# Compression's first layer as three f16 products a step, with keys and values split ahead of their copies

## The chip, the cores and the metric

The kernel runs on one core of a Trainium2 chip. The metric is the device time of one execution in microseconds (us), from the start of the program to its end; lower is better. A core has five engines with instruction queues of their own, each worked off in order: TensorE (PE in the profile, its weight loads PEld), VectorE (DVE), ScalarE (ACT), GpSimd (POOL) and SyncE (SP, which here only issues transfers). Transfers run on 16 DMA engines.

## The reference, cut to what matters

The program computes two transformer blocks for 256 tokens of width 1024. In the first block one branch is a sparse attention, which also attends to *compressed* keys and values: every 16 tokens a window of 32 tokens, with a position vector added to each token, is flattened and passed through a small two-layer network, once for keys (j = 0) and once for values (j = 1), in both groups g of heads:

```python
n_cmp = (T - CMP_BLOCK) // CMP_STRIDE + 1          # 15 windows
def compress(kx, j):
    blk = kx[:, :, cmp_idx] + pe_cmp[j]            # 32 tokens x 64
    flat = blk.reshape(B, G, n_cmp, CMP_BLOCK * dh)    # 2048 long
    return jax.nn.silu(flat @ w_cmp1[j]) @ w_cmp2[j]   # 2048 -> 128 -> 64
```

The change concerns `flat @ w_cmp1[j]`, a product of 2 x 15 rows of length 2048 with a 2048 x 128 matrix, for j = 0 and 1.

## The kernel before, in words

Nearly all products are made with numbers split in two f16 halves: a weight chunk of 1 MB arrives as f32 in a tile `raw` (pool `wraw`, four buffers), ACT writes its rounded half (`hi`, L194) and DVE the rest (`lo`, L195) into a tile `whl` (three buffers), in two steps of 128x1024 each, and PE adds up hi x hi, hi x lo and lo x hi (L215 to L217 where the weights are stationary, L236 to L238 where the activations are).

Compression's first layer is the exception: it is made in f32. `kv_pair(0, kvc)` (L472) writes keys and values of all tokens to `kvc` (ACT, L468, two instructions). The tile `k2` (L480, slot G23) is cleared by a DVE memset (L481), and four GpSimd transfers (L483, L484) lay the rows of `kvc` into it, for each group once as they are and once moved by one token, so that the 128 partitions hold two tokens of 64 values. A third plane of `k2` takes the position vectors, which two SyncE transfers (L563) write into every second element, 4 bytes at a time. The first-layer weights `w1` come by SyncE (L565) as 1 MB each, straight into two tiles `thg` of f32. A step k (L497) multiplies a 128x128 block of `w1` with 45 columns of `k2` (15 windows of two groups and 15 of the plane of position vectors), and 16 steps add up one j. `compress` (L502) then adds the column of the position vectors to the others (L504, L505), applies the nonlinearity and makes the second layer.

The order around it in the program's text: projection of keys and values (`kv_pair(0)`), queries 0 and 1 (`nq_pair(0)`, L561), the loads of position vectors and `w1` (loop at L562), queries 2 and 3 (`nq_pair(2)`), the other keys (`kv_pair(2, ksw)`, L568), then `projB('vsw', ...)` (L583), which makes a projection in 16 rounds of three matmuls and calls `two_steps` (L577) ahead of each round: two compression steps a round, 32 in all. An explicit edge (`issue_after`) keeps them behind `kv_op`, the last matmul of `kv_pair(2)`. After that come `compress` for both j, and the attention.

The kernel doesn't write out the queues' order otherwise: the framework lays the instructions of each engine out when it compiles, by the program's order and by what it thinks is ready, and adds the waits. So ACT's queue has work of later lines ahead of work of earlier ones (for instance squares of `memT`, L356, ahead of L468). Tiles with the same tag share a slot: the next user waits for the last reader. `e8` (L452), a small table that goes out by a GpSimd transfer (L455, `edr`), has the slot of `kvc`, so L468 waits for that transfer. The PSUM tiles `mm_ps` have two buffers, so `nq_pair(2)` can start only when L468 has emptied that of `kv_pair(0)`.

Of the kernel before, what the change touches and what calls it, by code (L numbers as in the profile page):

```python
# [8 lines left out]
F32 = mybir.dt.float32  # L9
F16 = mybir.dt.float16  # L10
I32 = mybir.dt.int32
AF = mybir.ActivationFunctionType
OP = mybir.AluOpType
# [4 lines left out]
T = 256  # L18
# [4 lines left out]
SW = 512.0  # L23
# [53 lines left out]
def trunk_kernel(ctx, tc, ap, off, dump=None):  # L77
    nc = tc.nc
    V, S, PE, G = nc.vector, nc.scalar, nc.tensor, nc.gpsimd
# [4 lines left out]
    wraw = ctx.enter_context(tc.tile_pool(name="wraw", bufs=4))  # L84
    wsp = ctx.enter_context(tc.tile_pool(name="wsp", bufs=3))
    act = ctx.enter_context(tc.tile_pool(name="act", bufs=1))
# [347 lines left out]
    nc.sync.dma_start(out=rows, in_=bass.AP(tensor=r_ap.tensor, offset=r_ap.offset, ap=[[0, 128], [1, NROW]]))  # L434
    smw = act.tile([128, 608], F32, name="smw", tag="Y").rearrange("p (k c) -> p k c", k=8)
    nc.sync.dma_start(out=smw, in_=ap['wsm'])
    smh = const.tile([128, 8, 56], F16, name="smh")
    sml = const.tile([128, 8, 56], F16, name="sml")
    split(smw[:, :, :56], smh, sml, SW)
# [37 lines left out]
    wc2 = const.tile([128, 2, 64], F32, name="wc2")  # L477
    nc.sync.dma_start(out=wc2, in_=ap['wcmp2'])
    cw1 = []
    k2 = act.tile([128, 2, 3, 272], F32, name="k2", tag="G23")  # L480
    V.memset(k2, 0.0)  # L481
    for g, gp in enumerate((slice(0, 64), slice(64, 128))):
        G.dma_start(out=k2[0:64, :, g, :T], in_=kvc[gp])  # L483
        G.dma_start(out=k2[64:128, :, g, :T - 1], in_=kvc[gp, :, 1:])  # L484
    ck2 = [k2[:, j] for j in range(2)]
    bt = act.tile([128, 8, T], F32, name="bt", tag="Q8")
    G.dma_start(out=bt, in_=bass.AP(tensor=edr.tensor, offset=edr.offset, ap=[[1, 128], [384, 8], [1, T]]))

    def compress_step(j):

        ps = sm_ps()[:, :45].rearrange("p (g c) -> p g c", g=3)
        k_ = [0]

        def step():
            k = k_[0]
            k_[0] += 1
            PE.matmul(ps, cw1[j][:, k * 128:k * 128 + 128], ck2[j][:, :, 2 * k:2 * k + 225:16],  # L497
                      start=k == 0, stop=k == 15)

        return ps, step  # L500

    def compress(j, ps):  # L502
        z = sm.tile([128, 45], F32, name="cz").rearrange("p (g c) -> p g c", g=3)
        V.tensor_copy(z[:, 2, 0:1], ps[:, 2, 0:1])  # L504
        V.tensor_scalar(z[:, 0:2], ps[:, 0:2], z[:, 2, 0:1], None, op0=OP.add)  # L505
        th = sm.tile([128, 2, 15], F32, name="cth")
        S.activation(out=th, in_=z[:, 0:2], func=AF.Tanh, scale=0.5)
        if j == 0:
            hd = sm.tile([128, 2, 15], F32, name="chd")
            V.scalar_tensor_tensor(hd, th, 1.0, z[:, 0:2], op0=OP.add, op1=OP.mult)  # L510
            ps = sm_ps()
# [48 lines left out]

    nq_pair(0)  # L561
    for j in range(2):  # L562
        nc.sync.dma_start(out=ck2[j][:, 2, 0:32:2], in_=ap['pe'][j])  # L563
        w1 = gpool.tile([128, 8, T], F32, name="thg").rearrange("p k t -> p (k t)")
        nc.sync.dma_start(out=w1, in_=ap['wc1'][j])  # L565
        cw1.append(w1)
    nq_pair(2)
    kv_op = kv_pair(2, ksw)  # L568
# [1365 lines left out]
```

## Time and profile before

| | |
|---|---|
| median of 3 runs | 917.85 us (914.5 to 918.71) |
| the profiled execution: time | 914.95 us |
| the profiled execution: span on the core | 913.2 us |
| TensorE busy | 885.0 us, 97% of the span |
| VectorE busy | 698.3 us, 76% |
| ScalarE busy | 539.1 us, 59% |
| GpSimd busy | 53.1 us, 6% |

The span is the time between the first and the last recorded instruction; 1.75 us of the execution lie around it. Each row of the timeline gives start, duration, engine, line and operation, output and inputs, shapes, and in brackets how long the engine was idle just before and what ended that. Matmuls are pipelined: the duration of one is its way through the array, and the rate at which they are worked off is read from the distance of their starts.

### The profile page before, as it was taken

To read this page: it belongs to the slowest core of one execution; us is meant where nothing else is said; L and a number is where in the kernel's file an instruction comes from. 1 tells how busy PE (TensorE), PEld (TensorE's weight loads), DVE (VectorE), ACT (ScalarE), POOL (GpSimd) and SP (SyncE) were. 2 spreads that over 40 slices of the span, in tenths; PEclk is the share of its full clock that TensorE was granted. 3 is DMA by queue.
4 is the path that set the end of the run, shared out by engine and by line. 5 is a ranking of instruction groups with operands and counts; after the bars stand their busy time and mean duration, and the time that the engine had idled before them with its cause. 6 is when DMAs were issued, how large, how long until landed. Compare 5 with 4: busy or idle time off the path is not lost. (4 is left out here: it accounts for less than half of the span.)

```text
span 913.2 us, 21140 instructions
## 1 busy us (share of the span) xinstructions
PE 885.0 (97%) x8843; PEld 758.1 (83%) x8843; DVE 698.3 (76%) x1484; ACT 539.1 (59%) x924; POOL 53.1 (6%) x61
## 2 busy tenths in 40 slices
PE   8899999999999999999999999999999999999995
PEld 6787687998888888888888888888888988777773
DVE  8768897767887667557998988767644888899994
ACT  7575947655565454444655765574345656597871
POOL 1310000000200000012000010000001000001102
PEclk9999999999999999999999999999999999999998
DMA  9881355365565565555545243456554666899991
GB/s 331 298 276 72 105 185 184 117 208 185 185 208 208 190 211 201 188 205 186 186 139 186 94 146 133 139 188 224 189 184 134 246 235 220 305 365 415 409 404 34
DMA packets 33331, 189.86 MB, mean 208 GB/s; under 512 B 7571, under 2 KB 7996, under 8 KB 11724
## 3 DMA queue, kind: packets, MB, share of 16 engines
q1 hardware_dynamic: 31004, 178.43, 54.6%
q0 software_dynamic: 2192, 9.97, 3.3%
q8 instruction: 71, 1.16, 0.5%
q14 instruction: 32, 0.26, 0.1%
q10 hardware_dynamic: 32, 0.03, 0.0%
HBM read 185.86 MB, written 2.37 MB: 206 GB/s over the span
## 5 line engine op out<-in xcount | busy, mean ns | idle before, releaser
L195 DVE SCALAR_TENSOR_TENSOR whl<-raw,whl 128x1024 f16<-128x1024 f32 (+1 forms) x264 | 313.2, 1210 | 68.8 <-ACT whl L194 67.2
L194 ACT ACTIVATE whl<-raw 128x1024 f16<-128x1024 f32 (+1 forms) x264 | 261.7, 1029 | 104.8 <-issue 51.6
L215 PE MATMUL mm_ps<-u,whl 128*128 128x256 f16 x792 | 216.6, 274 | 2.9 <-ACT whl L194 2.9
L217 PE MATMUL mm_ps<-u,whl 128*128 128x256 f16 x792 | 216.6, 273 | 0.9 <-DVE whl L195 0.9
L216 PE MATMUL mm_ps<-u,whl 128*128 128x256 f16 x792 | 216.6, 273 | 0.0
L215 PEld LDWEIGHTS <-whl 128*128 128x128 f16 x1768 | 174.7, 99 | 24.2 <-ACT whl L194 3.2
L217 PEld LDWEIGHTS <-whl 128*128 128x128 f16 x1768 | 173.3, 98 | 22.9 <-DVE whl L195 1.1
L216 PEld LDWEIGHTS <-whl 128*128 128x128 f16 x1768 | 173.3, 98 | 21.9 <-issue 1.8
L216 PE MATMUL mm_ps<-f,whl 128*128 128x256 f16 x352 | 95.9, 273 | 0.0
L217 PE MATMUL mm_ps<-f,whl 128*128 128x256 f16 x352 | 95.9, 273 | 0.0
L215 PE MATMUL mm_ps<-f,whl 128*128 128x256 f16 x352 | 95.9, 273 | 0.0
L998 ACT ACTIVATE gu_t<-mm_ps 128x256 f32<-128x256 f32 x22 | 8.5, 384 | 53.8 <-PE mm_ps L217 53.8
L236 PE MATMUL mm_ps<-whl,u 128*128 128x256 f16 x128 | 35.1, 275 | 0.0
L238 PE MATMUL mm_ps<-whl,u 128*128 128x256 f16 x128 | 34.9, 272 | 0.0
L237 PE MATMUL mm_ps<-whl,u 128*128 128x256 f16 x128 | 34.8, 272 | 0.0
L999 DVE SCALAR_TENSOR_TENSOR gu_t<-gu_t,mm_ps 128x256 f32<-128x256 f32 x22 | 9.2, 420 | 31.2 <-ACT gu_t L998 31.2
L338 POOL TENSOR_TENSOR sqa<-sqa,sq 128x512 f32<-128x512 f32 x8 | 13.8, 1728 | 306.5 <-ACT sq L356 306.4
L1751 PEld LDWEIGHTS <-ehid 128*80 128x80 f16 x132 | 14.6, 117 | 13.5 <-ACT ehid L294 2.0
L1705 PEld LDWEIGHTS <-whl 128*128 128x128 f16 x576 | 21.6, 100 | 3.5 <-issue 1.8
L215 PE MATMUL mm_ps<-mg,whl 128*128 128x256 f16 x64 | 17.4, 272 | 0.3 <-ACT mg L294 0.3
L216 PE MATMUL mm_ps<-mix,whl 128*128 128x256 f16 x64 | 17.4, 272 | 0.2 <-DVE mix L298 0.2
L215 PE MATMUL mm_ps<-mix,whl 128*128 128x256 f16 x64 | 17.1, 272 | 0.4 <-DVE gtmp L898 0.4
(610 smaller groups left out, 1836.2 us busy)
## 6 DMA issues: line engine op xcount, KB each, us to landing
raw<-in_w SPq DMA_DIRECT2D x138, 1024.0 KB, 4.9
raw_G<-in_w SPq DMA_DIRECT2D x9, 1024.0 KB, 6.6
raw_R<-in_w SPq DMA_DIRECT2D x5, 1024.0 KB, 7.3
raw_Y<-in_w SPq DMA_DIRECT2D x5, 1024.0 KB, 10.8
raw_K<-in_w SPq DMA_DIRECT2D x4, 1024.0 KB, 12.5
raw<-in_w SPq DMA_DIRECT2D x7, 512.0 KB, 7.4
thg<-in_wc SPq DMA_DIRECT2D x2, 1024.0 KB, 11.3
whl<-in_w POOLq DMA_DIRECT2D x2, 1024.0 KB, 9.7
```

Of the source, the lines that this page charges most:

```text
L194: S.activation(out=hi[:, p], in_=raw[:, p], func=AF.Copy, scale=SW)
L195: V.scalar_tensor_tensor(lo[:, p], raw[:, p], SW, hi[:, p], op0=OP.mult, op1=OP.subtract)
L215: PE.matmul(out, wh, xh[:, k0 + k], start=first and k == 0, stop=False)
L216: PE.matmul(out, wh, xl[:, k0 + k], start=False, stop=False)
L217: i = PE.matmul(out, wl, xh[:, k0 + k], start=False, stop=last and k == nk - 1)
L236: PE.matmul(ps[:, a, :w], xh[:, k, ts], hv[:, k], start=k == 0, stop=False)
L237: PE.matmul(ps[:, a, :w], xh[:, k, ts], lv[:, k], start=False, stop=False)
L238: PE.matmul(ps[:, a, :w], xl[:, k, ts], hv[:, k], start=False, stop=k == 7)
L338: self.eng.tensor_tensor(out=acc, in0=acc, in1=sq, op=OP.add)
L999: V.scalar_tensor_tensor(th, th, 1.0, ps[:, :T], op0=OP.add, op1=OP.mult)
L1705: unit_op[0] = PE.matmul(o, w_[:, b], xg[x_][:, g, k], stop=x_ == 1 and k == 7, start=w_ is hi and x_ == 0 and k == 0)
L1751: PE.matmul(dps[c], hh[:, x_, k], w_[:, k * D + c * 512:k * D + c * 512 + 512], start=e % 4 == 0 and k == 0 and i == 0, stop=e % 4 == 3 an ...
```

## The change

Each number of `kvc`, of the position vectors and of `w1` is split in an f16 half and a rest, and each compression step becomes three f16 matmuls (hi x hi, hi x lo, lo x hi) in place of one of f32, which the trace shows as two instructions. The weights' hi and lo are scaled by SW = 512, and `compress` takes the scale out. The splits are made by `split`: ACT writes hi (L294), DVE the rest (L296 for scale 1, L298 otherwise). `kvc` is split once, ahead of the four copies, into `kv16` (slot pct); the copies then move hi and lo of both j. `k2` is now f16, twice as many elements of half the size, and lies in slot K8 (next used by `xp`). The position vectors come in one transfer early in the program, contiguous, to a tile of their own, and are split into `k2`. `w1` arrives in the pool `wraw`, and four splits of 128x1024 write it into `thg`.

```diff
+    pe32 = sm.tile([128, 2, 16], F32, name="pe32", bufs=1)
+    nc.sync.dma_start(out=pe32, in_=ap['pe'].rearrange("j p c -> p j c"))
...
-    k2 = act.tile([128, 2, 3, 272], F32, name="k2", tag="G23")
+
+    kv16 = act.tile([128, 2, 2, T], F16, name="kv16", tag="pct")
+    split(kvc, kv16[:, 0], kv16[:, 1], 1.0)
+    k2 = act.tile([128, 2, 2, 3, 272], F16, name="k2", tag="K8")
     V.memset(k2, 0.0)
+    split(pe32, k2[:, 0, :, 2, 0:32:2], k2[:, 1, :, 2, 0:32:2], 1.0)
+    k2_ = k2.rearrange("p s j g t -> p (s j) g t")
+    kv_ = kv16.rearrange("p s j t -> p (s j) t")
     for g, gp in enumerate((slice(0, 64), slice(64, 128))):
-        G.dma_start(out=k2[0:64, :, g, :T], in_=kvc[gp])
-        G.dma_start(out=k2[64:128, :, g, :T - 1], in_=kvc[gp, :, 1:])
-    ck2 = [k2[:, j] for j in range(2)]
+        G.dma_start(out=k2_[0:64, :, g, :T], in_=kv_[gp])
+        G.dma_start(out=k2_[64:128, :, g, :T - 1], in_=kv_[gp, :, 1:])
...
-            PE.matmul(ps, cw1[j][:, k * 128:k * 128 + 128], ck2[j][:, :, 2 * k:2 * k + 225:16],
-                      start=k == 0, stop=k == 15)
+            for i, (w_, x_) in enumerate(((0, 0), (0, 1), (1, 0))):
+                PE.matmul(ps, cw1[j][:, w_, k * 128:k * 128 + 128], k2[:, x_, j, :, 2 * k:2 * k + 225:16],
+                          start=k == 0 and i == 0, stop=k == 15 and i == 2)
...
-        V.tensor_copy(z[:, 2, 0:1], ps[:, 2, 0:1])
-        V.tensor_scalar(z[:, 0:2], ps[:, 0:2], z[:, 2, 0:1], None, op0=OP.add)
+        V.tensor_scalar(z[:, 2, 0:1], ps[:, 2, 0:1], 1.0 / SW, None, op0=OP.mult)
+        V.tensor_scalar(z[:, 0:2], ps[:, 0:2], 1.0 / SW, z[:, 2, 0:1], op0=OP.mult, op1=OP.add)
...
     for j in range(2):
-        nc.sync.dma_start(out=ck2[j][:, 2, 0:32:2], in_=ap['pe'][j])
-        w1 = gpool.tile([128, 8, T], F32, name="thg").rearrange("p k t -> p (k t)")
-        nc.sync.dma_start(out=w1, in_=ap['wc1'][j])
+        raw = wraw.tile([128, 2048], F32, name="raw")
+        nc.sync.dma_start(out=raw, in_=ap['wc1'][j])
+        w1 = gpool.tile([128, 8, T], F32, name="thg").bitcast(F16).rearrange("p k t -> p (k t)")
+        w1 = w1.rearrange("p (s c) -> p s c", s=2)
+        for i in range(2):
+            split(raw[:, 1024 * i:1024 * i + 1024], w1[:, 0, 1024 * i:1024 * i + 1024],
+                  w1[:, 1, 1024 * i:1024 * i + 1024], SW)
         cw1.append(w1)
```

## Rows read from the trace of the kernel before

**Rows 1.** The page's first part: busy time, share of the span, instructions.

```profile
PE 885.0 (97%) x8843; PEld 758.1 (83%) x8843; DVE 698.3 (76%) x1484; ACT 539.1 (59%) x924; POOL 53.1 (6%) x61
```

**Rows 2.** Busy time by stretch: length, PE, PEld, DVE, ACT, POOL, granted clock, DMA share, GB/s.

```profile
40.00:60.00 20.00, 16.25 (x134) 13.54 (x132) 10.20 (x11) 10.54 (x16) 3.41 (x5) 0.91 0.68 198
60.00:80.00 20.00, 19.88 (x223) 18.13 (x222) 14.03 (x56) 10.46 (x19) 0.00 (x0) 1.00 0.66 262
80.00:100.00 20.00, 20.00 (x161) 14.23 (x160) 18.40 (x99) 18.35 (x65) 0.00 (x0) 1.00 0.15 53
```

**Rows 3.** PE's timeline: the stall, and the last matmul ahead of compression.

```profile
46.18 0.28 PE L215 MATMUL mm_ps<-u,whl 128*128 128x256 f16 x1 [2.88 <-ACT whl L194]
...
47.44 0.39 PE L217 MATMUL mm_ps<-u,whl 128*128 128x256 f16 x1 [0.87 <-DVE whl L195]
...
59.16 0.27 PE L217 MATMUL mm_ps<-u,whl 128*128 128x256 f16 x1
```

**Rows 4.** ACT's timeline at the stall.

```profile
44.34 0.84 ACT L468 ACTIVATE kvc<-mm_ps,cols 128x256 f32<-128x256 f32 x2 [8.78 <-DMA edr<-e]
45.07 2.00 ACT L194 ACTIVATE whl<-raw 128x1024 f16<-128x1024 f32 x2
```

**Rows 5.** PE's timeline: compression steps, first, second and last round of 16.

```profile
59.27 0.56 PE L497 MATMUL sm_ps<-k,thg 128*128 128x45 f32 x4
59.66 0.29 PE L236 MATMUL mm_ps<-whl,u 128*128 128x256 f16 x1
...
60.00 0.56 PE L497 MATMUL sm_ps<-k,thg 128*128 128x45 f32 x4
...
70.78 0.27 PE L238 MATMUL mm_ps<-whl,u 128*128 128x256 f16 x1
```

**Rows 6.** PE's timeline: first and last of 48 small f16 matmuls (L248 to L250).

```profile
75.94 0.18 PE L248 MATMUL sm_ps<-smh,u 128*128 128x32 f16 x1
...
77.13 0.18 PE L250 MATMUL sm_ps<-smh,u 128*128 128x32 f16 x1
```

**Rows 7.** Groups by shape, 40 to 78 us: weight loads and splits (busy us, mean ns, idle).

```profile
L195 DVE SCALAR_TENSOR_TENSOR whl<-raw,whl 128x1024 f16<-128x1024 f32 x11 | 13.1, 1223 | 11.7 <-ACT whl L194 11.7
L194 ACT ACTIVATE whl<-raw 128x1024 f16<-128x1024 f32 x12 | 12.2, 1052 | 7.5 <-DMA raw<-in_w 4.6 <-PE mm_ps L238 2.8
...
L248 PEld LDWEIGHTS <-u 128*128 128x128 f16 x16 | 1.3, 99 | 0.0
```

**Rows 8.** Timelines of ACT and DVE: one split of 128x512 to f16.

```profile
26.61 0.63 ACT L294 ACTIVATE u<-nrm_u 128x512 f16<-128x512 f32 x1 [2.47 <-DVE nrm_u L317]
...
27.28 0.69 DVE L296 TENSOR_TENSOR u<-nrm_u,u 128x512 f16<-128x512 f32 x1
```

**Rows 9.** Groups of DVE by shape: the memset of k2.

```profile
L481 DVE MEMSET k<- 128x1632 f32 x1 | 1.4, 1418 | 0.4 <-issue 0.4
```

**Rows 10.** DVE's timeline: last splits of the chunks of kv_pair(0) and nq_pair(0).

```profile
32.41 1.22 DVE L195 SCALAR_TENSOR_TENSOR whl<-raw,whl 128x1024 f16<-128x1024 f32 x1
...
36.99 1.21 DVE L195 SCALAR_TENSOR_TENSOR whl<-raw,whl 128x1024 f16<-128x1024 f32 x1
```

**Rows 11.** Transfers issued from 30 to 44 us: line, count, KB each, us to landing.

```profile
raw<-in_w SPq DMA_DIRECT2D x3, 1024.0 KB, 10.1
thg<-in_wc SPq DMA_DIRECT2D x1, 1024.0 KB, 13.4
```

**Rows 12.** Waits of SyncE's queue, 0 to 78 us: total, times, longest.

```profile
SPq L563 <- DMA k<-kvc: 20.0, 1, 20.0
```

**Rows 13.** POOL's timeline: transfer of edr, then the first copy of kvc.

```profile
38.73 0.75 POOL L455 DMA_DIRECT2D edr<-e  x1
...
45.51 0.64 POOL L483 DMA_DIRECT2D k<-kvc  x1
```

**Rows 14.** Transfers issued from 44 to 60 us: the copies of kvc, KB, us to landing.

```profile
raw<-in_w SPq DMA_DIRECT2D x4, 1024.0 KB, 8.4
...
k<-kvc POOLq DMA_DIRECT2D x2, 128.0 KB, 6.9
```

## The prediction

> **What bounds the kernel now.** I began with the page's busy times [rows 1]: TensorE works for 97% of the span, no other engine for more than 76%. So time is gained where PE gets less to do or waits less; work added to ACT or DVE is free as long as PE doesn't wait for it. The table by stretch shows that this holds around the change [rows 2]: from 60 to 80 us, where the compression steps run, PE is busy for 19.88 of 20 us, DVE for 14.03 and ACT for 10.46. From 40 to 60 us PE is busy for only 16.25, and the mean granted clock is 0.91, the lowest of the stretches that I print.
>
> PE's timeline shows why [rows 3]: ahead of 46.18 us it is idle for 2.88 us, waiting for the hi half of a weight chunk, and for 0.87 us more ahead of 47.44, waiting for the lo half. ACT's timeline gives the cause behind the named one [rows 4]: L468, which empties the PSUM tile of keys and values, stood for 8.78 us until the transfer of `edr` had read `e8`, whose slot `kvc` takes; the hi half of the next chunk (queries 2 and 3) came right behind it at 45.07. [...]
>
> From 47.44 us on PE goes through without a gap of note to the steps: the last matmul ahead of them starts at 59.16 [rows 3], the first step at 59.27 [rows 5]. Each of 16 rounds has two steps, that is four f32 instructions, and three f16 matmuls of the projection. From the start of the four to that of the three is 59.66 - 59.27 = 0.39 us, and the round takes 60.00 - 59.27 = 0.73 us.
>
> **The change part by part.**
>
> *Steps on PE.* Removed: 16 x 0.39 = 6.2 us. Added: 96 f16 matmuls with 128x128 weights and 45 columns. The trace doesn't have this shape; the nearest is a run of 48 f16 matmuls with 128x128 weights and 32 columns [rows 6], which start (77.13 - 75.94) / 47 = 0.0253 us apart, though each of their weight loads lasts 0.099 us [rows 7]: the loads overlap. From below: 96 x 0.0253 = 2.4 us. From above, each at a whole weight load: 96 x 0.099 = 9.5 us, which is a loss of 3.3 us. I take the lower end, since shape, type and engine are the same but for 13 columns, and both ends of that run are plain in the rows. The columns of `k2` are picked with a step of 16 elements in either version. So PE gains 6.2 - 2.4 = 3.8 us.
>
> [...]
>
> *Split of `kvc`.* ACT gets one instruction of 128x512, DVE one of the same shape: 0.63 and 0.69 us by such a split elsewhere [rows 8]. In the text it stands right behind L468, just where PE waits for ACT's next instruction [rows 4]. If it lies there, PE's restart moves by 0.63 us; if the chunk goes first, by nothing; if DVE's rest also stands ahead of the chunk's lo half, by up to 0.63 + 0.69 = 1.3 us. I take 0.6.
>
> *Splits of `w1`.* Four on ACT at 12.2 / 12 = 1.02 us, four on DVE at 1.2 us [rows 7]: 4.1 and 4.8 us. Their cover: ACT stands for 8.78 us ahead of 44.34 [rows 4], and DVE waits for ACT's halves for 11.7 us in all from 40 to 78 us [rows 7]. The loads are the same 2 MB as before, issued at the same place; one of them took 13.4 us to land before [rows 11], and should be no slower now that the 4-byte transfers of position vectors, which share the queue, are gone. I cost the splits at nothing. If ACT's four stood behind L468 and ahead of the next chunk, the cover would be gone and PE would restart 4.1 us later; the chunk of queries would be late next.
>
> *Buffers.* The two raw tiles of `w1` take two of four `wraw` buffers, so that of queries 2 and 3 now waits for the last split of `kv_pair(0)`, which starts at 32.41 us, and the next for that of `nq_pair(0)`, at 36.99 [rows 10]. With 1.2 us for the split and 10.1 us to land [rows 11] these are there at 43.7 and 48.3; the first was used at 45.07 [rows 4], the second after 48 more matmuls. Nothing, with 1.4 us to spare.
>
> *Copies.* The same bytes, in runs of 512 B where they had 1 KB. The first was issued at 45.51 [rows 13], right after L468; now it waits for both halves of `kv16`, so 45.2 + 0.63 + 0.69 = 46.5, and the last of four, 0.63 us apart, goes at 48.4. With 6.9 us to land [rows 14] they are there at 55.3, 4 us ahead of the first step. Nothing, as long as they land in under 11 us after the issue.
>
> *Position vectors.* SyncE stood for 20.0 us at the second of their transfers, until the copies had landed [rows 12], with weight loads queued behind it. That wait goes, since the early transfer waits for nothing of the kind. It was not on PE's path: ACT waited 4.6 us for a load behind it [rows 7], while PE had work. What is late next for those loads is a free `raw` buffer. The new transfer is small; its splits are 32 elements a partition.
>
> *Memset.* 1.4 us before [rows 9]. With twice the elements of half the size it takes between 1.4 and 2.8 us; it stands ahead of the first splits, and the wait for `edr` in front of the restart hides what it delays. The two scalings in `compress` take the place of two instructions of the same shape. The clearing of `xp`, which takes over slot K8, now waits for the last step, long ahead of its use. Nothing for all of these.
>
> *What follows behind.* The attention begins with what compression gives, so its work on DVE and ACT moves forward with the steps. From 80 to 100 us DVE has 18.40 and ACT 18.35 of 20 us [rows 2]: near full, but PE is full as well, so a start that is earlier for all three is kept.
>
> **Sum.** -3.8 + 0.6 = -3.2 us. Against the profiled execution, 914.95 - 3.2 = 911.7 us. That execution is 2.9 us under the median of three runs, and I forecast a median: 917.85 - 3.2 = 914.6 us. Its own range is 912.5 to 917, by 1.3 in place of 0.6 us for the split, and by some microseconds between executions (914.5 to 918.71 before). About 0.5%, or 4.6 us, is what a measurement here can tell from no change.
>
> **Rivals.**
>
> *Stall gone, 909.1 us.* With no wait for the copies in SyncE's queue and four more instructions in ACT's, the framework may order things so that `edr` goes out earlier: POOL issued it only at 38.73, with no idle time ahead of it [rows 13], so other work of POOL stood in front: the sums of squares that it gets from ACT. Then 2.88 + 0.87 us of idling and 1.8 us of clock go as well, 5.5 us at most. For it: ACT's new work stands ahead of those squares in the text. Against: no line of the diff touches `e8` or its transfer. 17%.
>
> *Splits of `w1` ahead of the queries' chunk, 918.7 us.* 914.6 + 4.1, as above. For it: in the text they stand there. Against: ACT's gap of 8.78 us is there to be filled with what is ready. 18%.
>
> *Copies land late, 923 us: slower.* The place is the first step, where PE's queue has the projection's 48 matmuls behind it. Before, SyncE stood still while they ran, and the weight loads issued from 44 to 60 us took 8.4 us [rows 14]; now those loads share the DMA engines with the copies. If the copies have twice the runs and so take 2 x 6.9, and a load's 8.4 on top, they land at 48.4 + 22.2 = 70.6, PE waits from 59.9 for 10.7 us, and the sum is 914.6 + 10.7 = 925; at half of that load 921, so 923 in the middle. It is slower than before from a landing 14.7 us after issue on. Against: the copies took 6.9 us before, and the weight loads of that time, freed from the queue, may be through by then. 9%. [...]
>
> *Weight loads one after another, 921.7 us.* The change then doesn't do what it says: six matmuls a round take 6 x 0.099 = 0.59 us where four instructions took 0.39, and 914.6 + 3.8 + 3.3 = 921.7. Against: [rows 6]. 8%. [...]
>
> **How the numbers follow.** The forecast has 48%. Faster by over 0.5% is under 913.3 us: nearly all of the first rival, and the lower part of the forecast's own range, 0.16 + 0.14 = 0.30. Slower by over 0.5% is over 922.4 us: most of the late copies and the upper part of the serial loads, 0.07 + 0.03 = 0.10. Within it: 0.60. The range runs from 909.0 to 921.5 us: half of the first rival, half of the last and most of the late copies lie outside, 0.08 + 0.04 + 0.08 = 0.20.
>
> **What would show it.** Right: a round of 0.49 us, 16 of them in 7.8 us; no idling of PE at the first step; L563's wait gone from SyncE's queue; ACT's splits of `w1` before L468. Wrong: PE idle for over 3.5 us ahead of the queries' chunk (splits in the way), or at the first step with the copies as its releaser (late copies), or rounds of 0.7 us and more (serial loads). The forecast also falls if the steps are shorter and PE waits by as much later, at the attention's first product or at a weight chunk.

## The result, and the profile after

The changed kernel takes 923.77 us (median of 4 runs, 922.2 to 924.37), the kernel before in the same comparison 918.28 us (914.5 to 918.94): a ratio of 1.008, 95% interval 1.0058 to 1.0103. It is slower by 0.8% by this ratio (the two medians are 5.5 us apart), where the forecast was a gain of 3.2 us. The ratios here and below are estimated from the executions within 1.5% of the fastest of their kernel; the medians are of all executions, and their quotients differ a little from the ratios (1.006 here). The profiled execution has a span of 920.0 us against 913.2, so 6.8 us have to be found. That is one execution of each kernel, and the one of the kernel before (914.95 us) is a fast one: the median of its four is 918.28.

Where they arise can be read from PE's timeline, by the start of the same work in both kernels:

| start on PE, us | before | after | later by |
|---|---|---|---|
| first compression step | 59.27 | 61.98 | 2.7 |
| last round of steps | 70.16 | 74.46 | 4.3 |
| small projection (L248) | 75.94 | 79.93 | 4.0 |
| transposes of smx | 130.64 | 136.71 | 6.1 |
| transposes of gr | 144.91 | 150.34 | 5.4 |
| transposes of gc, behind them | 149.90 | 157.08 | 7.2 |
| products with wrg | 767.77 | 774.90 | 7.1 |
| products of rawn_Q and eth | 865.32 | 873.22 | 7.9 |
| end of the span | 913.2 | 920.0 | 6.8 |

The page's first part answers to [rows 1]. TensorE is as full as before, and busy for longer.

```profile
PE 890.6 (97%) x8875; PEld 762.5 (83%) x8875; DVE 703.0 (76%) x1490; ACT 544.8 (59%) x930; POOL 53.9 (6%) x61
```

By stretches of 20 us (columns as in [rows 2]): from 40 to 60 us PE is busy for 14.43 us in place of 16.25 and the mean granted clock falls to 0.83 (it is 0.50 from 46.7 to 53.5 us). From 140 to 160 us the mean is 0.91, where it was 1.00 before: a second stretch at the lower clock (0.50 from 152.5 to 155.9 us), worth (1 - 0.91) x 20 = 1.8 us by an estimate from that mean. A third lies near the end: from 795 to 805 us the mean is 0.83 (0.50 from 797.7 to 801.0 us), where the kernel before has 1.00 at the same work (788 to 798 us).

```profile
40.00:60.00 20.00, 14.43 (x112) 12.02 (x110) 15.65 (x26) 13.98 (x20) 4.47 (x7) 0.83 0.91 306
...
140.00:160.00 20.00, 18.36 (x153) 15.53 (x151) 13.98 (x27) 13.17 (x24) 0.00 (x0) 0.91 0.46 154
...
795.00:805.00 10.00, 9.23 (x201) 8.76 (x198) 9.13 (x40) 2.60 (x8) 0.00 (x0) 0.83 0.69 258
```

PE's timeline at the restart and at the first steps answers to [rows 3, 5].

```profile
47.26 0.39 PE L215 MATMUL mm_ps<-u,whl 128*128 128x256 f16 x1 [4.09 <-ACT whl L194]
...
49.99 0.40 PE L217 MATMUL mm_ps<-u,whl 128*128 128x256 f16 x1 [1.48 <-DVE whl L195]
...
61.98 0.66 PE L505 MATMUL sm_ps<-k,thg 128*128 128x45 f16 x6
62.46 0.29 PE L236 MATMUL mm_ps<-whl,u 128*128 128x256 f16 x1
```

Two things are to be seen. The waits ahead of the queries' chunk are 4.09 and 1.48 us in place of 2.88 and 0.87. And six f16 step matmuls take 62.46 - 61.98 = 0.48 us, 0.080 us each: more than the 0.39 us of the four f32 instructions that they replace, and three times the 0.025 us of the sum. A round is 0.83 us (the next begins at 62.81) in place of 0.73.

ACT's timeline answers to [rows 4]. `edr` released the eviction (now L470) at 43.01, 1.3 us earlier than before, but between it and the chunk (L194) there now stand two of the four splits of `w1` (`thg`) and that of `kvc`. The first two `w1` splits, at 35.79, lie in the idle time, as predicted.

```profile
35.79 1.99 ACT L294 ACTIVATE thg<-raw 128x1024 f16<-128x1024 f32 x2
...
43.01 0.84 ACT L470 ACTIVATE kvc<-mm_ps,cols 128x256 f32<-128x256 f32 x2 [4.72 <-DMA edr<-e]
43.74 1.05 ACT L294 ACTIVATE thg<-raw 128x1024 f16<-128x1024 f32 x1
44.69 0.62 ACT L294 ACTIVATE kv<-kvc 128x512 f16<-128x512 f32 x1
45.20 1.05 ACT L294 ACTIVATE thg<-raw 128x1024 f16<-128x1024 f32 x1
46.15 2.00 ACT L194 ACTIVATE whl<-raw 128x1024 f16<-128x1024 f32 x2
```

DVE's timeline shows the same for the other half: two sums of squares and three splits ahead of the chunk's lo half at 48.71. DVE started on them late, after 3.19 us of waiting for a sum on POOL, which stood behind POOL's next transfer (`bt`, 43.21), and that one had waited 2.94 us for `edr` to land.

```profile
44.97 0.96 DVE L345 TENSOR_TENSOR sqa<-sqa,sq 128x256 f32<-128x256 f32 x2 [3.19 <-POOL sqa L340]
45.84 1.22 DVE L298 SCALAR_TENSOR_TENSOR thg<-raw,thg 128x1024 f16<-128x1024 f32 x1
46.98 0.68 DVE L296 TENSOR_TENSOR kv<-kvc,kv 128x512 f16<-128x512 f32 x1
47.58 1.22 DVE L298 SCALAR_TENSOR_TENSOR thg<-raw,thg 128x1024 f16<-128x1024 f32 x1
48.71 2.35 DVE L195 SCALAR_TENSOR_TENSOR whl<-raw,whl 128x1024 f16<-128x1024 f32 x2
```

POOL's timeline answers to [rows 13]. `edr` now goes out after one of the sums of squares in place of three, but that sum took 5.37 us.

```profile
32.47 5.37 POOL L338 TENSOR_TENSOR sqa<-sqa,sq 128x512 f32<-128x512 f32 x1 [28.02 <-ACT sq L356]
37.80 0.75 POOL L457 DMA_DIRECT2D edr<-e  x1
...
47.95 0.65 POOL L491 DMA_DIRECT2D k<-kv  x1 [3.02 <-DVE kv L296]
```

### The profile page after: what moved, and what is told of

It reads as the page before. It is cut to its first block, busy times and chain, and to the rows that moved or that the text cites. A ratio compares the mean times of both kernels' runs of the same rounds, so it can differ in the third digit from the quotient of the medians.

```text
span 920.0 us, 21215 instructions
## 1 busy us (share of the span) xinstructions
PE 890.6 (97%) x8875; PEld 762.5 (83%) x8875; DVE 703.0 (76%) x1490; ACT 544.8 (59%) x930; POOL 53.9 (6%) x61
## 5 line engine op out<-in xcount | busy, mean ns | idle before, releaser
L194 ACT ACTIVATE whl<-raw 128x1024 f16<-128x1024 f32 (+1 forms) x264 | 261.2, 1028 | 102.1 <-issue 48.9
L338 POOL TENSOR_TENSOR sqa<-sqa,sq 128x512 f32<-128x512 f32 x8 | 15.7, 1971 | 310.3 <-ACT sq L356 310.2
```

The source lines that it names most:

```text
L194: S.activation(out=hi[:, p], in_=raw[:, p], func=AF.Copy, scale=SW)
L338: self.eng.tensor_tensor(out=acc, in0=acc, in1=sq, op=OP.add)
```

## The experiments

All times in one table; the ratio is to the kernel before, run on the same chip beside them (its median was 916.97 us beside the first four experiments, 916.92 beside the next four and 916.37 beside the last four). A gain over the changed kernel is read below as the difference of two ratios; by their intervals such a difference is known to about 2.4 us (half widths of 0.22% and 0.14%, squared and added).

| run | median, us | ratio and 95% interval | span of the profile |
|---|---|---|---|
| changed kernel | 923.77 | 1.008 (1.0058 to 1.0103) | 920.0 |
| distances of the columns | 922.63 (one execution) | | 920.4 |
| adjacent columns | 918.75 | 1.0024 (1.0011 to 1.0038) | 915.6 |
| second w1 behind the chunk | 920.38 | 1.0035 (1.0022 to 1.0049) | 919.2 |
| both | 916.72 | 1.0006 (0.9991 to 1.002) | 913.7 |
| before, position vectors early | 912.95 | 0.9965 (0.9948 to 0.9982) | 908.8 |
| before, e8 in another slot | 917.67 | 1.002 (0.9991 to 1.005) | 914.2 |
| pairs, second w1 behind | 914.77 | 0.9977 (0.9962 to 0.9992) | 911.5 |
| the same, e8 in another slot | 912.67 | 0.996 (0.9946 to 0.9973) | 910.3 |
| changed, edr by SyncE | 919.39 | 1.0039 (1.0024 to 1.0054) | 917.7 |
| before, edr by SyncE | 925.67 | 1.0075 (1.0051 to 1.01) | 923.6 |
| before, vectors early and edr by SyncE | 933.71 | 1.0189 (1.0172 to 1.0206) | 924.0 |
| pairs, second w1 behind, edr by SyncE | 914.88 | 0.9994 (0.9978 to 1.001) | 912.4 |

**What a step matmul costs.** One run varies the distance of the columns, the weights and the number of columns.

```diff
+            q = (1, 2, 4, 8)[k // 4] if j == 0 else (16, 16, 16, 6)[k // 4]
+            m = slice(0, 1) if j == 1 and k // 4 == 1 else slice(0, 3)
-            for i, (w_, x_) in enumerate(((0, 0), (0, 1), (1, 0))):
+            for i, (w_, x_) in enumerate(((0, 0), (0, 1), (0 if j == 1 and k < 4 else 1, 0))):
-                PE.matmul(ps, cw1[j][:, w_, k * 128:k * 128 + 128], k2[:, x_, j, :, 2 * k:2 * k + 225:16],
+                PE.matmul(ps[:, m], cw1[j][:, w_, k * 128:k * 128 + 128],
+                          k2[:, x_, j, m, 2 * k:2 * k + 14 * q + 1:q],
```

> The changed kernel, with the six steps' matmuls altered step by step, so that one run measures the candidates side by side. For j = 0 the 15 columns of a window group are taken at a distance of 1 element (steps 0 to 3), 2 (4 to 7), 4 (8 to 11) and 8 (12 to 15) in place of 16. For j = 1 the distance is 16 as in the changed kernel, but steps 0 to 3 use one and the same weight block for their three matmuls, steps 4 to 7 multiply only one group (15 columns), steps 8 to 11 are unaltered, steps 12 to 15 have distance 6. It multiplies other columns of k2 than the reference does, so only the times of the rounds are read. In the changed kernel six matmuls take 0.48 us, 0.080 us each. Theory A (the distance of the moving columns sets the 80 ns): rounds with distance 1 have six matmuls in about 0.15 to 0.2 us (0.025 to 0.035 each, as the run of small matmuls of 32 adjacent columns), the price rises with the distance towards 0.08 at 16, the rounds with one group cost about a third (0.027 each), those with the same weights are no cheaper than 0.08. Theory B (weight loads one after another): all rounds of six loads take 0.48 us whatever the distance and the number of columns; only a load that could be left out would help. Theory C (a price per instruction, from the PSUM accumulation or the three groups): 0.08 at every distance.

PE's timeline, one round of each kind with the matmul that ends it: distance 1, 4, 8; then, for j = 1, distance 16 with the same weights three times, with 15 columns; then distance 6.

```profile
64.09 0.31 PE L507 MATMUL sm_ps<-k,thg 128*128 128x45 f16 x6
64.25 0.27 PE L236 MATMUL mm_ps<-whl,u 128*128 128x256 f16 x1
...
66.03 0.44 PE L507 MATMUL sm_ps<-k,thg 128*128 128x45 f16 x6
66.29 0.29 PE L236 MATMUL mm_ps<-whl,u 128*128 128x256 f16 x1
...
68.06 0.66 PE L507 MATMUL sm_ps<-k,thg 128*128 128x45 f16 x6
68.54 0.29 PE L236 MATMUL mm_ps<-whl,u 128*128 128x256 f16 x1
...
68.89 0.67 PE L507 MATMUL sm_ps<-k,thg 128*128 128x45 f16 x6
69.37 0.29 PE L236 MATMUL mm_ps<-whl,u 128*128 128x256 f16 x1
...
70.55 0.33 PE L507 MATMUL sm_ps<-k,thg 128*128 128x15 f16 x6
70.72 0.27 PE L236 MATMUL mm_ps<-whl,u 128*128 128x256 f16 x1
...
73.21 0.53 PE L507 MATMUL sm_ps<-k,thg 128*128 128x45 f16 x6
73.56 0.29 PE L236 MATMUL mm_ps<-whl,u 128*128 128x256 f16 x1
```

Six matmuls take 0.16 us at distance 1 (and 0.15 to 0.17 at 2), 0.26 at 4, 0.35 to 0.38 at 6, 0.48 at 8 and at 16, all at a granted clock of 1.00. The same weights save nothing (0.48); a third of the columns costs a third (0.17). So it is theory A, and more exactly: up to 8 elements (16 bytes) the price rises with the distance, at 8 and at 16 it is 0.080 / 45 = 1.8 ns a column, and the cheapest matmuls take some 26 ns each. Theories B and C are out: by them every distance would cost the same.

**Adjacent columns.** The splits write token 16 b + r to place 16 r + b, so a step's columns lie side by side.

```diff
+    perm = lambda t: t.rearrange("p j (r b) -> p j b r", r=16)
-    split(kvc, kv16[:, 0], kv16[:, 1], 1.0)
+    split(kvc.rearrange("p j (b r) -> p j b r", r=16), perm(kv16[:, 0]), perm(kv16[:, 1]), 1.0)
...
-        G.dma_start(out=k2_[64:128, :, g, :T - 1], in_=kv_[gp, :, 1:])
+        G.dma_start(out=k2_[64:128, :, g, :T - 16], in_=kv_[gp, :, 16:])
...
+            o = 2 * k % 16 * 16 + 2 * k // 16
-                PE.matmul(ps, cw1[j][:, w_, k * 128:k * 128 + 128], k2[:, x_, j, :, 2 * k:2 * k + 225:16],
+                PE.matmul(ps, cw1[j][:, w_, k * 128:k * 128 + 128], k2[:, x_, j, :, o:o + 15],
```

> The changed kernel with k2 laid out so that the 15 windows of a step lie next to each other: the two splits write token 16 b + r to place 16 r + b, and the copies for the upper partitions are moved by 16 places. Nothing else is changed. Theory A (distance of the moving columns): six matmuls of a round take 0.15 to 0.2 us in place of 0.48, 16 rounds gain 16 x 0.3 = 4.8 us, and the time falls from 923.8 to about 919; the splits of kv with strided writes may give 0.5 us back. Theory B (weight loads): rounds stay at 0.83 us, the time within 1 us of the changed kernel's.

A round is now 0.48 us (64.38 to 64.86), the six matmuls 0.15: 0.35 us less than in the changed kernel, 5.6 over 16 rounds. By the ratios the time falls by (1.008 - 1.0024) x 918 = 5.1 us. In the profiles the small projection comes at 76.68 in place of 79.93: the 5.6 us of the steps, less 2.4 by which they begin later. Of the rest of the 4.4 us between the spans, the stretch at the lower clock at the transposes of `gr` is the main part; this execution has 1.00 there. The same stream of weights as in the changed kernel runs at 25 ns a matmul, so loads one after another are no limit here. The price is at the split of `kvc`: with writes 32 bytes apart it takes 2.39 us on ACT and 2.35 on DVE where it took 0.62 and 0.68, both ahead of the queries' chunk, and PE restarts at 49.75, after a wait of 6.64 us.

```profile
45.51 2.39 ACT L294 ACTIVATE kv<-kvc 128x512 f16<-128x512 f32 x1
...
47.94 2.35 DVE L296 TENSOR_TENSOR kv<-kvc,kv 128x512 f16<-128x512 f32 x1
```

**The second w1 behind the chunk.** `chunk_ops` holds the last hi and the last lo split of the chunk made just before, here that of queries 2 and 3.

```diff
...
+    split_w1(0)
     nq_pair(2)
+    with tc.issue_after(chunk_ops[0].ins), tc.issue_after(chunk_ops[1].ins):
+        split_w1(1)
```

> The changed kernel, with the two splits of the second w1 (j = 1, ACT and DVE each 2 x 1024 columns) issued behind those of the queries' chunk that PE waits for. Theory R (the restart of PE is late because these splits and that of kv stand ahead of the chunk in ACT's and DVE's queues): PE's wait for the chunk's hi half falls from 4.09 to about 2 us, that for the lo half from 1.48 to about 0.5, the steps begin about 2 to 3 us earlier than at 61.98, and the time falls by 2 to 4 us, to some 921. Rival S (the chunk's arrival or edr sets the restart): the steps begin within 0.5 us of 61.98 and the time stays. Rival L (the delay is only moved: the second w1 is late at the 17th step): the restart is earlier, but PE waits for it in the middle of the rounds.

The time falls by (1.008 - 1.0035) x 918 = 4.1 us, within theory R, as far as a difference known to 2.4 us can tell. The profiled execution shows less of it (0.8 us of span), since there `edr` landed later (the eviction stands at 44.47, not 43.01). Measured from the eviction, the first step comes 61.01 - 44.47 = 16.5 us after it, where it was 61.98 - 43.01 = 19.0 in the changed kernel and 59.27 - 44.34 = 14.9 before [rows 4, 5]: 2.4 of 4.0 us are gone. The run with distances of the columns is the changed kernel up to its steps; there the way is 64.09 - 44.09 = 20.0 us, so one execution differs from another by 1 us in it, and by 2.1 us in the start of the first step. PE does not wait at the 17th step, so rival L is out.

```profile
46.98 0.40 PE L217 MATMUL mm_ps<-u,whl 128*128 128x256 f16 x1 [3.49 <-ACT whl L196]
...
47.94 0.34 PE L292 MATMUL at_ps<-ones,sqa 128*128 128x1 f32 x1 [0.35 <-DVE sqa L347]
```

**Both.**

> Both of the two edits before: adjacent columns and the second w1's splits behind the queries' chunk. Theories A and R together: the sum of the two gains, 4.8 + 2 to 4 = 7 to 9 us below the changed kernel, about 915 to 917, that is at or just under the kernel before (918.3). If the later losses (attention stretch, and a stretch at half clock at the transposes of the gathered scores, some 3 to 4 us) stay, nearer 919; if they hang on the late start, nearer 914.

916.72 us, level with the kernel before: by the ratios 6.8 us under the changed kernel, where the two gains alone come to 5.1 + 4.1 = 9.2. Whether they add up can't be told within the intervals.

**Position vectors alone.** The kernel before, f32 steps and all, with this one part of the change.

```diff
+    pe32 = sm.tile([128, 2, 16], F32, name="pe32", bufs=1)
+    nc.sync.dma_start(out=pe32, in_=ap['pe'].rearrange("j p c -> p j c"))
...
     V.memset(k2, 0.0)
+    V.tensor_copy(k2[:, :, 2, 0:32:2], pe32)
...
-        nc.sync.dma_start(out=ck2[j][:, 2, 0:32:2], in_=ap['pe'][j])
```

> The kernel before, with one part of the change alone: the position vectors come early in one contiguous transfer and a VectorE copy lays them into k2; the two SyncE transfers that waited for the copies of k2 are gone. Theory N (as predicted: that wait was not on PE's path): within 1 us of the kernel before, with SyncE's 20.0 us wait gone and the loads of weights earlier. Rival O (the order that the framework lays out changes as well, and with it the 2.1 us that the changed kernel and all its variants so far take longer from the small projection to the transposes of smx, 56.8 in place of 54.7 us): that stretch then takes about 56.8 us here too, and the time rises by 1 to 2 us.

Faster by 0.35%, against both expectations. POOL's and PE's timelines say how:

```profile
32.19 2.62 POOL L338 TENSOR_TENSOR sqa<-sqa,sq 128x512 f32<-128x512 f32 x1 [27.73 <-ACT sq L356]
34.75 0.75 POOL L457 DMA_DIRECT2D edr<-e  x1
```

```profile
44.25 0.28 PE L217 MATMUL mm_ps<-u,whl 128*128 128x256 f16 x1 [0.71 <-DVE whl L195]
...
54.52 0.56 PE L500 MATMUL sm_ps<-k,thg 128*128 128x45 f32 x4
```

The framework's order puts `edr` behind one sum of squares in place of three, as it does in the changed kernel, but here that sum takes 2.62 us: `edr` goes out at 34.75 in place of 38.73 [rows 13], the eviction comes at 41.15, PE idles for 0.71 us in all, there is no stretch at the lower clock, and the steps begin 4.75 us earlier. It is the rival called "stall gone". So the run prices the earlier `edr` together with the two transfers that are gone, and not either alone. Why the order changed with an edit that doesn't touch `edr` was not settled.

**e8 in another slot, in the kernel before.**

```diff
-    e8 = act.tile([8, 384], F32, name="e8", tag="kvc")
+    e8 = act.tile([8, 384], F32, name="e8", tag="K8")
```

> The kernel before, with the small table e8 in another free slot, so that the eviction of keys and values (L468) no longer waits for the transfer edr. It prices the stall that the prediction called 5.5 us at most: 2.88 and 0.87 us of idling ahead of the queries' chunk and 1.8 us of lower clock. Theory E (edr alone holds L468): the eviction comes at about 43 us, right behind the last matmul, the idling falls to under 1.5 us, no stretch at half clock, and the time falls by 3 to 5 us to some 912 to 914. Rival F (something else comes due just behind: the chunk's split, or the squares of memT on ACT): under 1.5 us gained.

A miss, for a reason of its own: slot K8 goes next to `xp`, and DVE's clearing of `xp` now waits for `edr`, with the chunk's lo half behind it. The eviction did come at 39.10, but the wait moved to another engine, and behind it lay the next one: the first step waits for the position vectors.

```profile
45.26 0.08 DVE L689 MEMSET xp<- 128x24 f32 x1 [4.40 <-DMA edr<-e]
```

```profile
46.92 0.28 PE L217 MATMUL mm_ps<-u,whl 128*128 128x256 f16 x1 [2.39 <-DVE whl L195]
...
59.38 0.63 PE L497 MATMUL sm_ps<-k,thg 128*128 128x45 f32 x4 [2.02 <-DMA k<-in_pe]
```

**Pairs.** A distance of 2 was as cheap as 1, so the splits may write in runs of two.

```diff
+    for j in range(2):
+        split(kvc[:, j].rearrange("p (b r i) -> p b r i", r=8, i=2),
+              kv16[:, 0, j].rearrange("p (r b i) -> p b r i", r=8, i=2),
+              kv16[:, 1, j].rearrange("p (r b i) -> p b r i", r=8, i=2), 1.0)
...
+            o = k % 8 * 32 + k // 8 * 2
+                PE.matmul(ps, cw1[j][:, w_, k * 128:k * 128 + 128], k2[:, x_, j, :, o:o + 29:2],
```

> As the run with adjacent columns and the second w1 behind the queries' chunk, but with k2 laid out in pairs: token 16 b + 2 r + i goes to place 32 r + 2 b + i, so the columns of a step are 2 elements apart (which took 0.15 to 0.17 us for six matmuls in the run with different distances) and the splits of kv write runs of 2 elements in place of 1. Theory W (the write with a distance of 32 bytes is what made the split of kv 2.36 us in place of 0.63 on ACT, and 2.35 on DVE, 1.7 us each on the way to the queries' chunk): with runs of two the splits take about 1.2 us each for all 512 columns, PE restarts 1 to 2 us earlier, and the time is 1 to 2 us under that run's 916.7. Rival X (a price per element, whatever the run): 2.4 us again, the same time within 0.5 us.

Theory W: the two halves take 0.73 us together on ACT and 1.29 on DVE, the steps begin at 61.20 in place of 63.53, and the time is 2.0 us lower. A round is 0.48 us, as with adjacent columns.

```profile
44.71 0.73 ACT L296 ACTIVATE kv<-kvc 128x256 f16<-128x256 f32 x2
...
45.16 1.29 DVE L298 TENSOR_TENSOR kv<-kvc,kv 128x256 f16<-128x256 f32 x2 [3.56 <-ACT kv L296]
```

**Pairs, and e8 in slot G23,** which is free in this version.

> The run before this one, and e8 in another slot so that the eviction of keys and values doesn't wait for edr. Theory: the gain of that edit alone in the kernel before (3 to 5 us) comes on top, some 911 to 913. Rival: ACT and DVE have more to do between the eviction and the chunk than before, so that not much over 2 us comes back.

912.67 us, 2.1 us better: the rival's size, but not its reason. The eviction is at 38.30, with the split of `kvc` and the chunk's hi halves right behind it, but POOL's next transfer, `bt`, which reads `edr`, still stands until that has landed, with the last sum of squares behind it. DVE and then PE wait for that (2.56 us).

```profile
43.22 0.97 POOL L500 DMA_DIRECT2D bt<-edr  x1 [2.84 <-DMA edr<-e]
44.21 0.75 POOL L342 TENSOR_TENSOR sqa<-sqa 128x256 f32<-128x256 f32 x1
```

```profile
46.02 0.63 PE L292 MATMUL at_ps<-ones,sqa 128*128 128x1 f32 x4 [2.56 <-DVE sqa L347]
```

**edr issued by SyncE,** in four versions: the changed kernel, the kernel before, that with the position vectors early, and the one with pairs.

```diff
-    G.dma_start(out=edr, in_=e8)
+    nc.sync.dma_start(out=edr, in_=e8)
```

> The changed kernel, with the transfer edr issued by SyncE in place of GpSimd, nothing else. Theory G (in the changed kernel edr is held back by GpSimd's sum sqa, 5.37 us in place of 2.6, and that holds the eviction of keys and values, so that the splits of w1 lose the idle time of ACT that should cover them): edr goes out at about 33 to 34 us, the eviction comes at about 39 to 40, right behind PE, ACT's two splits of the second w1 come before PE needs the chunk, PE idles for under 2.5 us in all ahead of the queries' chunk in place of 4.09 + 1.48, the steps begin 2.5 to 4 us earlier than at 61.98, and the time falls by 3 to 5 us to some 919 to 921. Rival (the splits themselves, two of ACT and two of DVE ahead of the chunk, are the delay, whatever edr does): PE's idle time stays over 4 us.

In the changed kernel the eviction comes at 38.52 and 3.8 us are gained by the ratios (1.008 to 1.0039). The waits are 0.29 and 2.74 us, more than theory G had: DVE is now the late one, with the splits of `kvc` and `w1` ahead of the chunk. The steps begin at 60.33, 1.65 us earlier than in the changed kernel's profile, where theory G had 2.5 to 4. So both the splits and `edr` have their share in the late restart.

```profile
47.31 0.39 PE L217 MATMUL mm_ps<-u,whl 128*128 128x256 f16 x1 [2.74 <-DVE whl L195]
```

> The kernel before, with the transfer edr issued by SyncE in place of GpSimd: the price of that wait alone, without the slot that the earlier attempt gave to e8 and that xp needs. Theory: eviction at about 39 us, idling ahead of the queries' chunk under 1 us in place of 2.88 + 0.87, no half clock, steps from about 55 us unless the position vectors hold them; then they wait for the second transfer of position vectors, as in the earlier attempt (2.02 us). Time 3 to 5 us under the kernel before without that second wait, 1 to 3 with it.

> The two edits together in the kernel before: position vectors early, and edr issued by SyncE; the steps remain in f32. It says what the f16 steps are worth beside it. Theory: as the run with the position vectors alone (span 908.8 us in the profile, median 912.95), or up to 1 us under it, since that run idled for only 0.71 us ahead of the chunk and had no half clock.

> The changed kernel with all that the runs so far found: columns in pairs, the second w1's splits behind the queries' chunk, and edr issued by SyncE. Theory: a round takes 0.49 us in place of 0.73 (f32) or 0.83 (changed), 3.8 us less than in f32 over 16 rounds; if PE's restart is as early as in the f32 version with position vectors and edr early, the time is 2 to 4 us under that version's, some 909 to 911. Rival: ACT and DVE have 2.4 and 2.6 us more to do for the splits of w1 and kv in this stretch and hold PE for as long, so that it comes out level with the f32 version, 912 to 913.

All three fall short of what was expected, and the second is 17 us slower than the kernel before (its profile is of its fastest execution, 926.19 us, and so shows only 10.8 of these in the span). In each the first step waits for the copies of `k2` or for the position vectors behind them:

```profile
58.29 1.06 PE L497 MATMUL sm_ps<-k,thg 128*128 128x45 f32 x4 [3.26 <-DMA k<-in_pe]
```

```profile
60.54 1.05 PE L500 MATMUL sm_ps<-k,thg 128*128 128x45 f32 x4 [6.58 <-DMA k<-kvc]
```

```profile
60.88 0.39 PE L512 MATMUL sm_ps<-k,thg 128*128 128x45 f16 x6 [4.09 <-DMA k<-kv]
```

With `edr` out of the way the copies are issued earlier, from 40.77, 39.87 and 43.35 us on, but they take 12.3 to 12.6, 17.3 to 18.0 and 13.8 to 14.7 us to land where they took 6.9 [rows 14]. Just ahead of them in POOL's queue goes `bt`, 1 MB, which takes 13.7, 16.0 and 12.0 us where it took 7.5; what each has to do with the other's delay was not separated. It is the rival "copies land late", met in other kernels than the one it was written for. In the two f32 versions the granted clock is lower as the steps begin (a mean of 0.52 from 58 to 60 us in the first, 0.56 from 56 to 60 in the second) and stays so: from 60 to 70 us it is 0.50 in both, and in the first the last round begins 20.4 us after the first step, 1.36 us a round. By the means it does not stay so for as long in every execution: the twelve of the first version take 916.38 to 931.03 us, at a mean granted clock from 0.995 down to 0.977 (0.984 in the profiled one). By stretches (columns as above), the first of the two:

```profile
58.00:60.00 2.00, 1.71 (x9) 1.61 (x10) 0.00 (x0) 0.00 (x0) 0.00 (x0) 0.52 0.82 328
60.00:70.00 10.00, 10.00 (x54) 9.07 (x54) 3.62 (x6) 4.70 (x7) 0.00 (x0) 0.50 0.82 343
70.00:78.00 8.00, 8.00 (x43) 7.20 (x44) 0.53 (x2) 0.00 (x0) 0.00 (x0) 0.50 0.39 131
```

## Why the prediction was wrong

The forecast was -3.2 us, the profile shows +6.8: 10 us between them (8.7 by the medians, which are 5.5 us apart). By the table of starts they go to the following terms, each read from one execution of either kernel.

*Steps on PE: -3.8 predicted, +1.6 measured.* This is the step that failed most, 5.4 us. It reads: "I take the lower end, since shape, type and engine are the same but for 13 columns". The run of small matmuls [rows 6] reads adjacent columns; these read every sixteenth. The prediction even said that "the columns of `k2` are picked with a step of 16 elements in either version", and gave it no price. 96 matmuls at 0.080 us are 7.7 us, not 2.4. The rival "weight loads one after another" came near in its time (921.7), but not in its mechanism: the same weights three times cost as much, and adjacent columns, with the same stream of weights as in the changed kernel, cost 25 ns. Whether the f32 steps of the kernel before, which read at 64 bytes' distance, would gain by the same layout no run shows.

*Splits ahead of the chunk: +0.6 predicted, +2.7 measured* (at the first step). "I cost the splits at nothing" (of `w1`) held for the first two of four. The other two stood between the eviction and the chunk, with the split of `kvc`, on ACT and on DVE. It was not room that they lacked: the second `w1` was issued at 25.1 us and no `raw` load up to 50 us took over 9.3 to land, and ACT stood for 4.72 us right ahead of the eviction. The sum took an idle gap as free for whatever is ready, but the eviction, which waited for `edr`, stood ahead of these splits in ACT's queue, and they ran only behind it, at 43.74 and 45.20. The rival that had all four there got 18%; its mechanism came true by half. With the second `w1` issued behind the chunk, 2.4 us of the way from eviction to first step are gone and 4.1 us of the time. The 2.7 is of one execution; in the run with distances of the columns, the same kernel up to there, the first step comes 4.8 us later than before.

*Two more stretches at the lower clock: not foreseen, 1.8 and 0.8 us.* The 1.8 us of clock in the rival "stall gone" are the stretch of the kernel before, an estimate from its mean in [rows 2]: (1 - 0.91) x 20. The trace shows a clock of 0.50 there from 47.3 to 50.7 us, 3.4 us; in the changed kernel neighbouring f16 matmuls of 256 columns start 0.21 us apart at 0.50 (50.17 to 50.81) and 0.11 at 1.00 (61.65 to 61.98), so by an estimate about half of these 3.4 us is lost. Of the two new ones, one follows the waits at the transposes of `gr`, the other lies at 795 to 805 us. From 140 to 160 us the profiles of the changed kernel, of the second `w1` behind the chunk and of pairs with `e8` elsewhere all show 0.91, those with adjacent columns and with pairs alone 1.00, and PE waits there for the same 1.64 us in all of them (1.65 in one). The kernel before waits for 1.87 us there and has 1.00; with `e8` in another slot, f32 steps and all, it waits for 1.88 and has 0.91. So it comes without f16 steps too. What decides it is open, and it may be the execution and not the change: of 31 executions of the kernel before, beside the second four experiments, 21 have a mean granted clock of 0.991 to 0.994 and take 917.5 us on average, three have 0.997 or 0.998 and take 913.1. The profiled one has 0.995.

*The order of the attention: not foreseen, 1.4 us.* From the small projection to the transposes of `smx` the changed kernel takes 56.8 us in place of 54.7. This isn't the f16 steps' doing: the two f32 versions with `edr` by SyncE take 56.8 as well, that with the position vectors alone 54.7. It isn't more work either: both have 485 matmuls in it, for which PE is busy 56.23 us in place of 54.58, and it idles for 0.55 in place of 0.12 (columns as in [rows 2]). Up to the transposes of `gr` 0.7 of the 2.1 come back. The two timelines have them in another order; why this one takes longer is open.

```profile
75.94:130.64 54.70, 54.58 (x485) 41.22 (x485) 49.55 (x206) 40.01 (x119) 0.59 (x1) 1.00 0.31 102
```

```profile
79.93:136.71 56.78, 56.23 (x485) 41.65 (x485) 49.57 (x198) 40.44 (x119) 0.56 (x1) 1.00 0.29 98
```

Together 5.4 + 2.1 + 1.8 + 0.8 + 1.4 = 11.5. Off this go 0.3 between the last round and the small projection, 0.1 in the long middle of the program and 1.1 at its very end, which no run explains: 10.0.

*Position vectors: nothing predicted, a gain that the change didn't get.* The wait of SyncE's queue [rows 12] did go. "It was not on PE's path" holds for that wait, but not for the edit: alone it brought 0.35%, in a profile in which `edr` had moved forward in POOL's order. In the changed kernel the same order was worth 0.9 us (37.80 in place of 38.73), since the sum ahead of it took 5.37 us in place of 2.62.

*What was right.* The copies in time in the changed kernel (no wait at the first step); the memset at 1.42 us, near the start; the first two `w1` splits in ACT's gap; buffers at no cost that PE shows.

A version that beats both kernels came out of it: f16 steps with columns in pairs, the second `w1` behind the chunk, and `e8` out of the slot of `kvc`, 912.67 us, 0.4% under the kernel before. The position vectors alone, with f32 steps, are level with it at 912.95.

## What to carry to other kernels

Before a matmul is priced by another one in the trace, compare the distance of its moving columns as well as shape and type: laid out in pairs, 96 f16 matmuls of 45 columns cost a third of what they cost at 32 bytes' distance (0.15 to 0.17 us for six at a distance of 2 elements, 0.48 at 16), and the layout can be made where the data is written, in runs of two. Splits and casts that an edit adds are free only if they stand in a gap of their engine: read which instruction ends the gap, since what stood behind it in the queue ran only after it here (the second `w1` was split behind the eviction, ahead of which ACT had stood for 4.72 us), and put whatever is not needed at once behind it by an explicit edge. And where a wait is to be taken away, ask what was hidden behind it: here three waits lay within a few microseconds (`edr`, the position vectors, the copies), and in the kernel before, taking away `edr` alone gained nothing (1.002, in another slot) or cost time (1.0075, by SyncE). Last, read a term from more than one execution before it is put down to a change: between two that are the same up to there, the first step moved by 2.1 us.

## What the runs showed of the hardware beside that

*Writes at a distance cost too.* The split of 128x512 elements took 0.62 us on ACT and 0.68 on DVE written side by side, 2.39 and 2.35 with each element 32 bytes from the last, 0.73 and 1.29 (in two parts; 0.75 on DVE in the two later runs with pairs) with runs of two.

*Issued earlier is not landed earlier.* The four copies took 6.9 us when they were issued from 45.5 us on, after 2 us in which the DMA engines moved nothing (44 to 46 us in the kernel before), and 17.3 to 18.0 when they were issued from 39.9 us on (vectors early and `edr` by SyncE), in a stretch (40 to 60 us) in which those engines were full, with a share of 1.00 and 358 GB/s.

*The lower clock can stay.* With the waits of 3.26 and 6.58 us just ahead of the f32 steps the clock went down to 0.50 and stayed there through all of the 16 rounds in the first case (until about 82 us) and through most of them in the second (until about 77), with PE busy all the while from the first step on. After the 4.09 us ahead of the f16 steps in pairs (with `edr` by SyncE) its mean from 60 to 80 us was 0.91, and neighbouring matmuls of the projection started 0.22 us apart up to 64.1 us and 0.11 from 64.5 on. In the kernel before the clock was back at 1.00 some 3.4 us after the fall (47.3 to 50.7 us). What tells the cases apart was not tested.

*A sum on POOL twice as long.* The first sum of squares took 5.37 us in the changed kernel, where DVE ran three splits with two inputs in a row (3.49 us at 33.23), and 2.62 where DVE had other work between them. Whether the one made the other longer no run isolated.
